# A hybrid decoder block: layer norm's sums kept group by group while the convolution runs

## The chip, the cores and the metric

The kernel runs on one core of a Trainium2 chip. The metric is the time of one execution on the device, in microseconds (us); lower is better. The kernel before took 1765.69 us, the median of three runs (1760.31 to 1766.15).

The core's engines run side by side, each working through its own queue in order: TensorE (PE, matmuls), VectorE (DVE), ScalarE (ACT), GpSimd (POOL) and SyncE (SP, which here only issues DMAs). An instruction that waits holds up whatever stands behind it in its queue.

## The reference

One decoder block over 256 positions of 2048 channels, all in float32. The part that the change touches is the causal convolution branch:

```python
def layernorm(x, g, b):
    mu = jnp.mean(xf, axis=-1, keepdims=True)
    var = jnp.mean(jnp.square(xf - mu), axis=-1, keepdims=True)
    y = (xf - mu) * lax.rsqrt(var + EPS) * g + b
...
def conformer_conv(glu_in, w_dw, b_dw, ln_g, ln_b, w_pw, b_pw):
    a, g = jnp.split(glu_in, 2, axis=-1)
    u = a * jax.nn.sigmoid(g)
    u = causal_dwconv(u, w_dw, b_dw)          # 31 taps, each channel alone
    u = jax.nn.silu(layernorm(u, ln_g, ln_b)) # over the 2048 channels
    return u @ w_pw + b_pw
...
proj = h @ w_in[l]                            # queries, keys, values, GLU input, merge gates
merged = jax.nn.sigmoid(ga) * y_a + jax.nn.sigmoid(gb) * y_b
x = x + g1 * (merged @ w_out[l])              # g1: a third of c_act @ w_ada's adaLN rows
```

Behind it stand a gated MLP and a final norm.

## The kernel before

**Weights and matmuls.** Every product streams its weights as tiles of 128x1024 (`wtile`): one DMA into `raw`, a rounded copy `hi` by ACT (L227), the remainder `lo` by DVE (L228). The pools hold four `raw` and three `hi` and `lo`, so `lo` of tile k can only be made once the matmuls of tile k-3 are over. A tile gives 12 matmuls of 512 columns (L249 to L251) in the products that this text speaks of. The tiles are counted here from 1 through the program: 187 to 218 are the merge gates of the convolution branch (`C_MB`), 219 to 250 the pointwise product `conv_pw_w`, which needs the whole normalised convolution `uT`, and 251 to 282 the product `w_out`.

**The convolution.** `u` holds the 2048 channels as 16 blocks of 128 (channels on partitions, 256 positions side by side). `conv_blocks` works on groups of 3, 3, 3, 3, 3 and 1 blocks: a tap is either one DVE instruction on one block (L549) or a product by ACT (L559) that DVE adds for the whole group (L568); the last tap writes the group back into `u` (L566). The running sum is the tile `cacc`, of which the pool holds two.

**Layer norm.** Sums over channels are sums over blocks (DVE) and then a matmul with ones (PE), which leaves the same sum on every partition. `ln_mean1` to `ln_mean4` add up all blocks, `ln_centre` subtracts the mean from four blocks at a time, squares them (ACT) and adds the squares up, `ln_var` makes 1/sqrt(variance) (one matmul, a square root on ACT, six small DVE instructions), `ln_scale` multiplies, `ln_silu` applies gain, bias and SiLU (ACT, block by block), `ln_split` makes `hi` and `lo` of the result for the matmuls (L350 on ACT, L351 on DVE).

**The adaLN rows.** `c_act @ w_ada` is done on DVE, one step (L298 or L301, on a tile of 128x1024 that has its own DMA, `araw`, two buffers) for each 128 rows. The 32 steps for `g1` are put in the queue by `conv_done`, when the convolution's pool is given back; `w_out`'s results need them. Others (`shift` and `scale` of the MLP) wait in the same queue.

**What sets the order.** Three queues of closures, `heads_q`, `conv_q` and `ada_q`, are dealt out by `tick` at each weight tile, by estimated loads; `norm_only` keeps `ada_q` back as long as `conv_q` still has steps. `drain(conv_q)` (L961) empties it when the gates' product has been issued. A scheduler then fixes each engine's order. All of that happens when the program is built.

## Time and profile before

| | |
|---|---|
| median of three runs | 1765.69 us (1760.31 to 1766.15) |
| the profiled execution | 1763.86 us, its span 1762.1 us |
| mean granted TensorE clock | 0.983 of full speed |
| busy: PE, DVE, ACT, POOL | 96%, 75%, 56%, 0% of the span |
| HBM traffic | 403.85 MB read, 2.10 MB written |

The span is what the profiler's records cover; the execution's own time is 1.8 us longer. A busy share is a mean over stages with different limits, and PE's is taken with matmul ends that are modelled: a full row says that matmuls followed each other without a gap. What a change in one stage is worth is read there, from which wait ends last. A wait is put down to the instruction whose end released it.

### The profile page before, as it was taken

How to read it: one execution, taken by the hardware profiler on the slowest of the kernel's cores; microseconds unless marked ns; L12 is line 12 of the kernel's file. 1: busy time of each engine (PE TensorE's matmuls, PEld its weight loads, DVE VectorE, ACT ScalarE, POOL GpSimd, SP SyncE). 2: the span in 40 equal slices, each digit the busy share in tenths (PEclk: the TensorE clock that was granted, in tenths of full speed). 3: DMA queues.
4: the chain of work that ended last, by engine and by line, in shares of the span. 5: the costliest groups of instructions: out<-in, count | busy, mean ns of one | idle time of the engine just before them, and what ended most of it. 6: DMA issues, size and time to landing. Idle time of an engine off the chain costs nothing.

```text
span 1762.1 us, 26526 instructions
## 1 busy us (share of the span) xinstructions
PE 1696.0 (96%) x10148; PEld 1468.2 (83%) x10148; DVE 1315.4 (75%) x1722; ACT 992.1 (56%) x1506; POOL 6.2 (0%) x28
## 2 busy tenths in 40 slices
PE   6999999999999999987999899999999999999997
PEld 4899999999887778865877888888988888898886
DVE  2677698898878899988897677776577776576665
ACT  4443576885677778755344565554455554345553
POOL 0000000000000000000000000000000000000000
PEclk8999999999999999998999999999999999999998
DMA  9999788877557346778898577776677765566653
GB/s 342 321 352 321 233 276 273 269 249 215 178 163 245 131 150 209 238 227 279 312 315 298 180 229 225 221 223 221 223 225 222 220 215 180 191 191 189 189 191 124
DMA packets 264362, 407.68 MB, mean 231 GB/s; under 512 B 12684, under 2 KB 156844, under 8 KB 263596
## 3 DMA queue, kind: packets, MB, share of 16 engines
q1 hardware_dynamic: 261676, 399.44, 69.9%
q10 hardware_dynamic: 2560, 6.55, 1.1%
q8 instruction: 79, 1.29, 0.3%
q14 instruction: 47, 0.39, 0.1%
HBM read 403.85 MB, written 2.10 MB: 230 GB/s over the span
## 4 chain that ended last, share of the span: by engine, by line
PE 87%; DMA 5%; DVE 4%; ACT 2%; issue 2%; SPq 0%; ACTq 0%; DVEq 0%
PE accp L282 18%; PE accx L250 12%; PE accx L249 11%; PE accx L251 11%; PE accp L283 9%; PE accw L261 6%; PE accw L264 6%; PE accw L263 6%; DMA araw<-in_w_ada_dram 3%; DVE t L301 1%; PE pt L788 1%; DVE lo L228 1%; PE pt L421 1%; PE pt L827 1%; DMA araw<-in_w_kc_dram 1%
## 5 line engine op out<-in xcount | busy, mean ns | idle before, releaser
L227 ACT CAST hi<-raw 128x1024 fp32r<-128x1024 f32 x546 | 572.1, 1048 | 639.7 <-PE accx L251 266.7
L228 DVE TENSOR_TENSOR lo<-raw,hi 128x1024 fp32r<-128x1024 f32 x546 | 665.5, 1220 | 317.8 <-ACT hi L227 314.3
L282 PE MATMUL accp<-act,hi 128*128 128x512 f32 x1408 | 495.5, 397 | 0.2
L249 PE MATMUL accx<-hi,act 128*128 128x512 f32 (+2 forms) x1176 | 429.1, 366 | 18.3 <-ACT act L350 17.7
L250 PE MATMUL accx<-lo,act 128*128 128x512 f32 (+2 forms) x1176 | 435.0, 370 | 3.9 <-DVE lo L228 3.7
L251 PE MATMUL accx<-hi,act 128*128 128x512 f32 (+2 forms) x1176 | 429.3, 365 | 0.8 <-DVE act L351 0.8
L283 PE MATMUL accp<-act,lo 128*128 128x256 f32 x1408 | 395.2, 281 | 0.2 <-DVE lo L228 0.2
L282 PEld LDWEIGHTS accp<-act,hi 128*128 128x128 f32 x1408 | 264.2, 188 | 64.1 <-DVE act L351 0.8
L249 PEld LDWEIGHTS accx<-hi,act 128*128 128x128 f32 x1176 | 222.8, 189 | 55.1 <-ACT act L350 18.6
L283 PEld LDWEIGHTS accp<-act,lo 128*128 128x128 f32 x1408 | 266.0, 189 | 0.8 <-DVE lo L228 0.6
L261 PE MATMUL accw<-act,hi 128*128 128x256 f32 x896 | 259.1, 290 | 4.9 <-ACT accw L587 2.8
L250 PEld LDWEIGHTS accx<-lo,act 128*128 128x128 f32 x1176 | 222.9, 190 | 45.3 <-DVE lo L228 9.7
L263 PE MATMUL accw<-act,hi 128*128 128x256 f32 x896 | 258.0, 288 | 0.0
L264 PE MATMUL accw<-act,lo 128*128 128x256 f32 x896 | 257.6, 288 | 0.2 <-DVE lo L228 0.2
L251 PEld LDWEIGHTS accx<-hi,act 128*128 128x128 f32 x1176 | 223.0, 190 | 36.7 <-issue 1.7
L261 PEld LDWEIGHTS accw<-act,hi 128*128 128x128 f32 x896 | 174.8, 195 | 11.7 <-issue 3.9
L264 PEld LDWEIGHTS accw<-act,lo 128*128 128x128 f32 x896 | 174.5, 195 | 3.9 <-issue 3.1
L263 PEld LDWEIGHTS accw<-act,hi 128*128 128x128 f32 x896 | 174.6, 195 | 3.5 <-issue 3.0
L301 DVE SCALAR_TENSOR_TENSOR t<-araw,cs,t 128x1024 f32<-128x1024 f32 x120 | 153.5, 1279 | 19.2 <-DMA araw<-in_w_ada_dram 18.9
L559 ACT ACTIVATE cprod<-big,cw 128x230 f32<-128x230 f32 (+27 forms) x298 | 124.6, 487 | 13.4 <-DVE cacc L568 11.3
L568 DVE TENSOR_TENSOR cacc<-cacc,cprod 128x726 f32<-128x726 f32 (+28 forms) x110 | 87.6, 797 | 11.4 <-ACT cprod L559 8.2
L549 DVE SCALAR_TENSOR_TENSOR cacc<-big,cw,cacc 128x232 f32<-128x232 f32 (+24 forms) x182 | 77.6, 463 | 0.6
(208 smaller groups left out, 1051.2 us busy)
## 6 DMA issues: line engine op xcount, KB each, us to landing
araw<-in_w_ada_dram SPq DMA_DIRECT2D x192, 512.0 KB, 5.0
raw<-in_w_in_dram SPq DMA_DIRECT2D x180, 512.0 KB, 4.9
raw<-in_ffn_w_up_dram SPq DMA_DIRECT2D x176, 512.0 KB, 4.5
raw<-in_ffn_w_down_dram SPq DMA_DIRECT2D x88, 512.0 KB, 3.7
raw<-in_w_o_nsa_dram SPq DMA_DIRECT2D x32, 512.0 KB, 3.7
raw<-in_conv_pw_w_dram SPq DMA_DIRECT2D x32, 512.0 KB, 5.6
raw<-in_w_out_dram SPq DMA_DIRECT2D x32, 512.0 KB, 5.2
araw<-in_w_kc_dram SPq DMA_DIRECT2D x8, 512.0 KB, 5.6
```

The source lines that it names most:

```text
L227: nc.scalar.copy(hi[:, :n], raw[:, :n])
L228: los.append(nc.vector.tensor_tensor(lo[:, :n], raw[:, :n], hi[:, :n], op=ALU.subtract).ins)
L249: nc.tensor.matmul(o, act[:, k, 0, s], hi, start=k == 0, stop=False)
L250: nc.tensor.matmul(o, act[:, k, 0, s], lo, start=False, stop=False)
L251: nc.tensor.matmul(o, act[:, k, 1, s], hi, start=False, stop=k == nk - 1)
L261: nc.tensor.matmul(acc[:, b, :], hi[:, s], act[:, k, 0, :], start=begin and k == first and b % 2 == 0, stop=False, skip_group_check=True)
L263: nc.tensor.matmul(acc[:, b, :], hi[:, s], act[:, k, 1, :], start=False, stop=False, skip_group_check=True)
L264: nc.tensor.matmul(acc[:, b, :], lo[:, s], act[:, k, 0, :], start=False, stop=last, skip_group_check=True)
L282: nc.tensor.matmul(acc[:, b], hi[:, s], act[:, k], start=k == 0, stop=False, skip_group_check=True)
L283: nc.tensor.matmul(acc[:, b, 0, :], lo[:, s], act[:, k, 0, :], start=False, stop=k == KB - 1, skip_group_check=True)
L301: nc.vector.scalar_tensor_tensor(acc, raw, cs[:, k:k + 1], acc, op0=ALU.mult, op1=ALU.add)
L559: nc.scalar.mul(box["p"][:, b - b0, s:], u[:, b, :T - s], cw[:, CW - 1 - s, b:b + 1])
```

## The change

The sums move into the convolution. After each group of `conv_blocks`, `norm_sums` subtracts a pivot from the group's blocks (`less`), squares them on ACT, and adds values and squares, 256 positions each, to the two halves of a tile `sq` (`add`). The pivot is the mean over the first group's 384 channels (`find`, once, with a matmul). At the end `ln_var` has one matmul with ones over both halves of `sq`: it makes the mean (less the pivot) and the variance as mean square less squared mean. `ln_scale` now subtracts the mean and multiplies. `ln_mean1` to `ln_mean4` and `ln_centre` are gone. `cacc` has one buffer where it had two, and the pool holds `sq` and `pivot` beside it. `norm_only` is set in `ln_var` and no longer in `conv_done`, which comes behind it; steps of `conv_q` that are dealt while it is set get a high priority, as those of `heads_q` have.

```diff
-            if q is heads_q:
+            if q is heads_q or q is conv_q and norm_only[0]:
                 es.enter_context(tc.high_priority(HP))
...
+    sq = cvp.tile([P, 2, T], F32, name="sq")
+    pivot = cvp.tile([P, T], F32, name="pivot")
+
+    def norm_sums(b0, n):
+        def sums(dst, a, fresh):
+            if fresh:
+                nc.vector.tensor_add(dst, a[:, 0, :], a[:, 1, :])
+            for j in range(2 if fresh else 0, n):
+                nc.vector.tensor_add(dst, dst, a[:, j, :])
+        def find():
+            sums(sq[:, 0, :], u[:, :n, :], True)
+            p_ = pt([P, T])
+            nc.tensor.matmul(p_, ones, sq[:, 0, :], start=True, stop=True)
+            nc.scalar.mul(pivot, p_, 1.0 / (n * P))
+        def less():
+            v = u[:, b0:b0 + n, :]
+            nc.vector.tensor_tensor(v, v, pivot[:, None, :].to_broadcast([P, n, T]), op=ALU.subtract)
+        def add():
+            v = u[:, b0:b0 + n, :]
+            s4 = t4([P, n, T])
+            nc.scalar.activation(s4, v, AF.Square)
+            sums(sq[:, 0, :], v, b0 == 0)
+            sums(sq[:, 1, :], s4, b0 == 0)
+        if b0 == 0:
+            conv_q.append(({"dve": 900, "act": 450, "pe": 250}, find))
+        conv_q.append(({"dve": 170 + n * 265}, less))
+        conv_q.append(({"dve": 840 * n, "act": 250 + 200 * n}, add))
...
-                    box["a"] = cvp.tile([P, n, T], F32, tag="cacc", name=nm("cacc"), bufs=2)
+                    box["a"] = cvp.tile([P, n, T], F32, tag="cacc", name=nm("cacc"))
...
+        norm_sums(b0, n)
...
     def conv_done():
         cv.__exit__(None, None, None)
-        norm_only[0] = True
...
     def ln_var():
+        norm_only[0] = True
+        vp = pt([P, 2, T])
+        nc.tensor.matmul(vp.rearrange("p a t -> p (a t)"), ones, sq.rearrange("p a t -> p (a t)"), start=True, stop=True)
         ve = t4([P, 4, T])
+        nc.vector.tensor_scalar(ve[:, 3, :], vp[:, 0, :], 1.0 / D, None, op0=ALU.mult)
+        nc.vector.tensor_mul(ve[:, 2, :], ve[:, 3, :], ve[:, 3, :])
+        nc.vector.scalar_tensor_tensor(ve[:, 0, :], vp[:, 1, :], 1.0 / D, ve[:, 2, :], op0=ALU.mult, op1=ALU.subtract)
+        nc.vector.tensor_scalar(ve[:, 0, :], ve[:, 0, :], EPS, None, op0=ALU.add)
...
     def ln_scale(j):
         def f():
             v = u[:, 4 * j:4 * j + 4, :]
+            nc.vector.tensor_tensor(v, v, lb["m"][:, None, :].to_broadcast([P, 4, T]), op=ALU.subtract)
             nc.vector.tensor_tensor(v, v, lb["r"][:, None, :].to_broadcast([P, 4, T]), op=ALU.mult)
...
+    conv_q.append(({"dve": 5500, "act": 500}, ln_var))
+    conv_q.append(({}, conv_done))
     conv_q.extend(({"dve": d, "act": a}, f) for d, a, f in
-                  [(1130, 0, ln_mean1), (1130, 0, ln_mean2), (1130, 0, ln_mean3), (900, 0, ln_mean4)]
-                  + [(2000, 1050, ln_centre(j)) for j in range(4)] + [(3000, 1700, ln_var)]
-                  + [(1130, 0, ln_scale(0))]
-                  + [i for j in range(4) for i in [(1130, 0, ln_scale(j + 1))] * (j < 3)
-                     + [(0, LN_SILU, ln_silu(4 * j)), (0, LN_SILU, ln_silu(4 * j + 2))]])
+                  [i for j in range(4) for i in [(2260, 0, ln_scale(j))]
+                   + [(0, LN_SILU, ln_silu(4 * j)), (0, LN_SILU, ln_silu(4 * j + 2))]])
```

The order that the scheduler makes of it is read at three places, all on DVE. In the changed kernel the lines of `conv_blocks` and `ln_*` have moved: L583, L602 and L600 are L549, L568 and L566; L553 is `less`, L543 an addition of `add`, L926 and L927 are `ln_scale`.

The first place is the hand-over to the last group of the convolution (one block). Before, at tiles 196 to 198 (`cacc_6793` is the running sum of blocks 12 to 14, `cacc_7423` that of block 15):

```order
L228 TENSOR_TENSOR lo_7661<-raw_7659,hi_7660 128x1024
L301 SCALAR_TENSOR_TENSOR t_1138_7313<-araw_7708,cs,t_1138_7313 128x1024
L568 TENSOR_TENSOR cacc_6793<-cacc_6793,cprod_7394 128x3x227
L568 TENSOR_TENSOR cacc_7423<-cacc_7423,cprod_7468 128x254
L228 TENSOR_TENSOR lo_7691<-raw_7689,hi_7690 128x1024
L566 TENSOR_TENSOR big_268<-cacc_6793,cprod_7417 128x768
```

and in the changed kernel, at tiles 208 to 210 (`cacc_7044` and `cacc_7739`):

```order
L228 TENSOR_TENSOR lo_7923<-raw_7921,hi_7922 128x1024
L602 TENSOR_TENSOR cacc_7044<-cacc_7044,cprod_7644 128x3x227
L600 TENSOR_TENSOR big_268<-cacc_7044,cprod_7667 128x768
L228 TENSOR_TENSOR lo_7953<-raw_7951,hi_7952 128x1024
L553 TENSOR_TENSOR big_268<-big_268,pivot 128x768
L228 TENSOR_TENSOR lo_7980<-raw_7978,hi_7979 128x1024
L301 SCALAR_TENSOR_TENSOR t_1132_7291<-araw_8030,cs,t_1132_7291 128x1024
L583 SCALAR_TENSOR_TENSOR cacc_7739<-big_268,cw,cacc_7739 128x250
```

The last group no longer starts beside the one in front of it, and the write-back of blocks 12 to 14 has moved from tile 197 to tile 208.

The second place is DVE's queue from `lo` of tile 221, the last that can be made ahead of the `conv_pw_w` product. Before (`t_1259_7920` is the tile in which `ln_var` works, `t_1296_8159` the sum of the first adaLN steps for `g1`; the row ahead of the first one is `lo` of tile 220 with L911 behind it):

```order
L228 TENSOR_TENSOR lo_8237<-raw_8235,hi_8236 128x1024
L914 TENSOR_TENSOR t_1259_7920<-t_1259_7920 128x256
L301 SCALAR_TENSOR_TENSOR t_1296_8159<-araw_8182,cs,t_1296_8159 128x1024
L915 TENSOR_TENSOR t_1259_7920<-t_1259_7920 128x256
L301 SCALAR_TENSOR_TENSOR t_1296_8159<-araw_8208,cs,t_1296_8159 128x1024
L916 TENSOR_SCALAR t_1259_7920<-t_1259_7920 128x256
L917 TENSOR_TENSOR t_1259_7920<-t_1259_7920 128x256
L923 TENSOR_TENSOR big_268<-big_268,t_1259_7920 128x1024 x4
```

and in the changed kernel (`cprod` are ACT's last products, `pt_8056` is the result of the one matmul):

```order
L228 TENSOR_TENSOR lo_8258<-raw_8256,hi_8257 128x1024
L602 TENSOR_TENSOR cacc_7739<-cacc_7739,cprod_7997 128x229
L602 TENSOR_TENSOR cacc_7739<-cacc_7739,cprod_8000 128x228
L602 TENSOR_TENSOR cacc_7739<-cacc_7739,cprod_8003 128x227
L600 TENSOR_TENSOR big_268<-cacc_7739,cprod_8006 128x256
L553 TENSOR_TENSOR big_268<-big_268,pivot 128x256
L543 TENSOR_TENSOR sq<-sq,big_268 128x256
L543 TENSOR_TENSOR sq<-sq,t_1279_8052 128x256
L911 TENSOR_SCALAR t_1281_8058<-pt_8056 128x256
L926 TENSOR_TENSOR big_268<-big_268,t_1281_8058 128x1024 x2
```

Behind these rows come L912, two more L926, L913 and L914, the reciprocal (L916), four small instructions (L917 to L920), the four L927 and the four L351; no L301 stands among them. The convolution's last four additions, its sums and all of `ln_var` have moved behind `lo` of tile 221. Before, the last write-back stood at tile 208 and the variance's matmul behind tile 218.

The third place is the product `w_out`, where the adaLN steps for `g1` end. Before, at tiles 259 to 262:

```order
L228 TENSOR_TENSOR lo_9156<-raw_9154,hi_9155 128x1024
L301 SCALAR_TENSOR_TENSOR t_1138_7313<-araw_9071,cs,t_1138_7313 128x1024
L228 TENSOR_TENSOR lo_9174<-raw_9172,hi_9173 128x1024
L1010 TENSOR_TENSOR t_1491_9143<-accx_8963,gb 128x512 x2
L301 SCALAR_TENSOR_TENSOR t_1138_7313<-araw_9074,cs,t_1138_7313 128x1024
L228 TENSOR_TENSOR lo_9192<-raw_9190,hi_9191 128x1024
```

and in the changed kernel, from tile 261 on (tiles 259 and 260 have two L301 each):

```order
L228 TENSOR_TENSOR lo_9223<-raw_9221,hi_9222 128x1024
L301 SCALAR_TENSOR_TENSOR t_1429_8890<-araw_8971,cs,t_1429_8890 128x1024
L301 SCALAR_TENSOR_TENSOR t_1429_8890<-araw_8974,cs,t_1429_8890 128x1024
L301 SCALAR_TENSOR_TENSOR t_1429_8890<-araw_8977,cs,t_1429_8890 128x1024
L228 TENSOR_TENSOR lo_9254<-raw_9252,hi_9253 128x1024
L301 SCALAR_TENSOR_TENSOR t_1132_7291<-araw_9053,cs,t_1132_7291 128x1024
L327 TENSOR_TENSOR gb<-pt_8981,gb 128x512
L327 TENSOR_TENSOR gb<-pt_8984,gb 128x512
L301 SCALAR_TENSOR_TENSOR t_1132_7291<-araw_9081,cs,t_1132_7291 128x1024
L351 TENSOR_TENSOR act_8216<-pt_9046,act_8216 128x2x256
L351 TENSOR_TENSOR act_8216<-pt_9074,act_8216 128x2x256
L301 SCALAR_TENSOR_TENSOR t_1132_7291<-araw_9102,cs,t_1132_7291 128x1024
```

The steps for `g1` begin behind `lo` of tile 230 instead of tile 220, and ten adaLN steps stand behind the four `lo` of tiles 259 to 262, where three stood. From tile 222 to tile 271 there are 41 steps, where there were 35.

## Rows read from the trace of the kernel before

**Rows 1.** The page's first part: span, busy time of each engine.

```profile
span 1762.1 us, 26526 instructions
...
PE 1696.0 (96%) x10148; PEld 1468.2 (83%) x10148; DVE 1315.4 (75%) x1722; ACT 992.1 (56%) x1506; POOL 6.2 (0%) x28
```

**Rows 2.** Stretches: us, PE, PEld, DVE, ACT, POOL busy (instructions), PEclk, DMA share, GB/s.

```profile
760.00:780.00 20.00, 20.00 (x89) 16.28 (x88) 17.80 (x22) 12.02 (x13) 0.00 (x0) 1.00 0.61 190
780.00:800.00 20.00, 4.58 (x21) 3.46 (x19) 16.58 (x18) 11.44 (x16) 0.00 (x0) 0.74 0.65 219
800.00:820.00 20.00, 18.02 (x67) 13.92 (x68) 16.93 (x15) 11.71 (x16) 0.00 (x0) 0.83 0.70 223
```

**Rows 3.** Timeline, PE: start, length, instruction [idle before].

```profile
784.19 0.39 PE L251 MATMUL accx<-hi,act 128*128 128x512 f32 x1
800.87 0.80 PE L249 MATMUL accx<-hi,act 128*128 128x512 f32 x1 [16.29 <-ACT act L350]
```

**Rows 4.** Timeline, DVE, the same stretch.

```profile
783.70 0.42 DVE L911 TENSOR_SCALAR t<-pt 128x256 f32<-128x256 f32 x1
...
785.92 1.75 DVE L913 RECIPROCAL t<-t 128x256 f32<-128x256 f32 x1 [1.14 <-ACT t L912]
...
790.80 1.28 DVE L301 SCALAR_TENSOR_TENSOR t<-araw,cs,t 128x1024 f32<-128x1024 f32 x1 [0.55 <-DMA araw<-in_w_ada_dram]
...
794.12 0.43 DVE L917 TENSOR_TENSOR t<-t 128x256 f32<-128x256 f32 x1
794.58 4.63 DVE L923 TENSOR_TENSOR big<-big,t 128x1024 f32<-128x1024 f32 x4
```

**Rows 5.** Timeline, ACT, the same stretch.

```profile
785.47 0.42 ACT L912 ACTIVATE t<-t 128x256 f32<-128x256 f32 x1
...
786.84 1.28 ACT L959 ACT_TABLE_LOAD   x1
788.13 1.02 ACT L959 ACTIVATE big<-accx 128x1024 f32<-128x1024 f32 x1
...
795.84 4.04 ACT L929 ACTIVATE big<-big,par 128x256 f32<-128x256 f32 x8 [5.39 <-DVE big L923]
799.78 1.03 ACT L350 CAST act<-big 128x1024 fp32r<-128x1024 f32 x1
```

**Rows 6.** Timeline, DVE, end of the convolution.

```profile
736.73 1.43 DVE L568 TENSOR_TENSOR cacc<-cacc,cprod 128x241 f32<-128x241 f32 x3
...
751.46 0.42 DVE L566 TENSOR_TENSOR big<-cacc,cprod 128x256 f32<-128x256 f32 x1
```

**Rows 7.** Timeline, ACT, end of the convolution.

```profile
738.17 1.26 ACT L559 ACTIVATE cprod<-big,cw 128x237 f32<-128x237 f32 x3
```

**Rows 8.** Timeline, PE, a 512-column float32 matmul with ones.

```profile
849.46 1.88 PE L326 MATMUL pt<-t,ones 128*128 128x512 f32 x4
```

**Rows 9.** Two more stretches, from the restart to w_out's second chunk.

```profile
815.50:951.30 135.80, 131.82 (x581) 104.39 (x579) 116.79 (x121) 53.70 (x59) 0.00 (x0) 1.00 0.92 324
816.00:830.00 14.00, 12.89 (x56) 10.11 (x55) 8.19 (x8) 4.21 (x4) 0.00 (x0) 1.00 1.00 378
```

**Rows 10.** DVE's groups there: busy us, mean ns, idle before, releaser.

```profile
L228 DVE TENSOR_TENSOR lo<-raw,hi 128x1024 fp32r<-128x1024 f32 x46 | 55.8, 1219 | 6.9 <-ACT hi L227 6.9
L301 DVE SCALAR_TENSOR_TENSOR t<-araw,cs,t 128x1024 f32<-128x1024 f32 x33 | 42.3, 1281 | 10.7 <-DMA araw<-in_w_ada_dram 10.7
```

**Rows 11.** Timeline, DVE: adaLN steps in and after the stop.

```profile
799.12 2.60 DVE L301 SCALAR_TENSOR_TENSOR t<-araw,cs,t 128x1024 f32<-128x1024 f32 x2
...
815.46 1.28 DVE L301 SCALAR_TENSOR_TENSOR t<-araw,cs,t 128x1024 f32<-128x1024 f32 x1
```

**Rows 12.** DMA issues there: KB each, median us to landing.

```profile
araw<-in_w_ada_dram SPq DMA_DIRECT2D x34, 512.0 KB, 5.2
```

**Rows 13.** Timeline, PE: a stop near 229 us.

```profile
229.13 0.39 PE L261 MATMUL accw<-act,hi 128*128 128x256 f32 x1 [2.76 <-ACT accw L587]
```

**Rows 14.** Timeline, PE: a stop near 610 us.

```profile
610.40 0.62 PE L822 MATMUL pt<-ident,s 128*128 128x128 f32 x2 [1.81 <-ACT s L817]
```

More of the change, by code (lines that the diff above doesn't have):

```diff
@@ L866, in conv_done @@
             ada_q.extendleft(reversed(ada_steps(2 * D + i * WT, to_bcast(gate1["b"], 2 * D, i), 1500)))
-    conv_q.append(({}, conv_done))
     lb = {}
-    def half_sum(dst, a):
-        nc.vector.tensor_add(a[:, 0:2, :], a[:, 0:2, :], a[:, 2:4, :])
-        nc.vector.tensor_add(dst, a[:, 0, :], a[:, 1, :])
-    def ln_mean1():
-        lb["a"] = t4([P, 4, T])
-        nc.vector.tensor_add(lb["a"], u[:, 0:4, :], u[:, 4:8, :])
-    def ln_mean2():
-        nc.vector.tensor_add(lb["a"], lb["a"], u[:, 8:12, :])
@@ L885, in ln_mean3 @@
-    def ln_mean3():
-        nc.vector.tensor_add(lb["a"], lb["a"], u[:, 12:16, :])
-    def ln_mean4():
-        half_sum(lb["a"][:, 0, :], lb["a"])
-        mp = pt([P, T])
-        nc.tensor.matmul(mp, ones, lb["a"][:, 0, :], start=True, stop=True)
-        lb["m"] = mp
-        lb["q"] = t4([P, 4, T])
-    def ln_centre(j):
-        def f():
-            v = u[:, 4 * j:4 * j + 4, :]
-            nc.vector.scalar_tensor_tensor(v, lb["m"][:, None, :].to_broadcast([P, 4, T]), -1.0 / D, v,
-                                           op0=ALU.mult, op1=ALU.add)
-            s4 = t4([P, 4, T])
-            nc.scalar.activation(s4, v, AF.Square)
-            half_sum(lb["q"][:, j, :], s4)
-        return f
@@ L905, in ln_var @@
     def ln_var():
-        q = lb["q"]
-        half_sum(q[:, 0, :], q)
-        vp = pt([P, T])
-        nc.tensor.matmul(vp, ones, q[:, 0, :], start=True, stop=True)
+        norm_only[0] = True
+        vp = pt([P, 2, T])
+        nc.tensor.matmul(vp.rearrange("p a t -> p (a t)"), ones, sq.rearrange("p a t -> p (a t)"), start=True, stop=True)
         ve = t4([P, 4, T])
-        nc.vector.tensor_scalar(ve[:, 0, :], vp, 1.0 / D, EPS, op0=ALU.mult, op1=ALU.add)
-        nc.scalar.activation(ve[:, 1, :], ve[:, 0, :], AF.Sqrt)
@@ L913, in ln_var @@
-        nc.vector.reciprocal(ve[:, 2, :], ve[:, 1, :])
-        nc.vector.tensor_mul(ve[:, 3, :], ve[:, 2, :], ve[:, 2, :])
-        nc.vector.tensor_mul(ve[:, 3, :], ve[:, 3, :], ve[:, 0, :])
-        nc.vector.tensor_scalar(ve[:, 3, :], ve[:, 3, :], -0.5, 1.5, op0=ALU.mult, op1=ALU.add)
-        nc.vector.tensor_mul(ve[:, 3, :], ve[:, 3, :], ve[:, 2, :])
-        lb["r"] = ve[:, 3, :]
+        nc.vector.tensor_scalar(ve[:, 3, :], vp[:, 0, :], 1.0 / D, None, op0=ALU.mult)
+        nc.vector.tensor_mul(ve[:, 2, :], ve[:, 3, :], ve[:, 3, :])
@@ new lines, in ln_var @@
+        nc.vector.scalar_tensor_tensor(ve[:, 0, :], vp[:, 1, :], 1.0 / D, ve[:, 2, :], op0=ALU.mult, op1=ALU.subtract)
+        nc.vector.tensor_scalar(ve[:, 0, :], ve[:, 0, :], EPS, None, op0=ALU.add)
+        nc.scalar.activation(ve[:, 2, :], ve[:, 0, :], AF.Sqrt)
+        nc.vector.reciprocal(ve[:, 1, :], ve[:, 2, :])
+        nc.vector.tensor_mul(ve[:, 2, :], ve[:, 1, :], ve[:, 1, :])
+        nc.vector.tensor_mul(ve[:, 2, :], ve[:, 2, :], ve[:, 0, :])
+        nc.vector.tensor_scalar(ve[:, 2, :], ve[:, 2, :], -0.5, 1.5, op0=ALU.mult, op1=ALU.add)
@@ L920, in ln_scale @@
+        nc.vector.tensor_mul(ve[:, 2, :], ve[:, 2, :], ve[:, 1, :])
+        lb["m"], lb["r"] = ve[:, 3, :], ve[:, 2, :]
     def ln_scale(j):
```

## The prediction

> **What bounds the kernel now.** I read the page's busy times first, then the span cut into stretches, then the timelines of PE, DVE and ACT where PE stops. PE is busy for 1696.0 of 1762.1 us [rows 1]: time comes or goes only where PE stops. In nearly all stretches it has 20.00 of 20 us, as from 760 to 780 [rows 2], 89 matmuls of 512 columns: 0.225 us each, 2.7 us for a weight tile's twelve. The one large stop lies at the change: 4.58 busy us from 780 to 800 at a granted clock of 0.74. PE issues the last matmul of the gates (tile 218) at 784.19 and the next (tile 219, which needs `uT`) at 800.87, idle for 16.29 us until ACT's first cast of `uT` [rows 3]. In between, DVE and ACT finish layer norm. The last DVE piece in front of SiLU is `ln_scale`, from 794.58 [rows 4]; ACT has waited 5.39 us for it when SiLU starts at 795.84, and PE starts 5.03 us after that [rows 3, 5].
>
> From there to 951 us PE loses another 4.0 us (131.82 of 135.80), in a stretch where the DMA engines are busy for 0.92 of the time and DVE for 116.79 us [rows 9]: the adaLN steps for `g1` share both with the weights. DVE waited 10.7 us there for their DMAs [rows 10].
>
> **What decides the change: where the convolution ends.** The second `cacc` is gone. Before, block 15's chain of 30 dependent taps ran beside blocks 12 to 14 and was written back at tile 208. Now it starts after them, with 2.7 us per tile of which `lo` takes 1.14 (four instructions of that size take 4.63 us [rows 4], so starts lie 1.14 apart); three taps take 1.43 [rows 6]. So three taps go with each tile and PE keeps its pace, but the last three land behind `lo` of tile 221. That `lo` cannot be made before the matmuls of tile 218 end, at 784.4. Hence the rest of the convolution and all of `ln_var` run while PE stands still, whatever the engines did earlier.
>
> **The stop, step by step**, with PE ending at 784.4 as before:
> - `hi` of tile 221 takes 1.05 on ACT and `lo` 1.14 on DVE, to 786.65. ACT makes the last gate (1.02 [rows 5]) and four products (1.26 for three [rows 7]): 788.15. The three additions and the write-back (0.42 [rows 6]) follow them: 788.75.
> - `less`, the addition of the values, ACT's square, the addition of the squares: 0.42 to 0.45 each, all dependent or nearly so: 790.1.
> - One matmul over 512 columns. Four records of that kind took 1.88 us, two for one matmul [rows 8]: 0.9 at the full clock. PE has then been idle for 5.7 us. After 16.29 idle us the first matmul took 0.80 where 0.39 is usual [rows 3], the lower level; so the bounds are 0.9 and 1.8. I take 1.7, as after the only long stop that I have a row of: 791.8.
> - L911 (0.34 to the next start), two subtractions of 1024, L912, two more subtractions, L913 and L914: 4 x 1.14 + 4 x 0.36 = 6.0, so 797.8. That is the order's doing: the four subtractions stand in front of the variance. The square root 0.5 [rows 5], the reciprocal 1.7 [rows 4], four small instructions at 0.42 on average (0.43 one, 0.46 to the next start [rows 4]): 801.7. The first L927 takes 1.26 until SiLU can start (794.58 to 795.84): 803.0.
> - From there 5.03 us to PE's first matmul: 808.0, against 800.87.
>
> So the stop grows by **7.1 us**; with the matmul at 0.9 it is 6.3. What falls away is in that: the variance's chain before took 12.1 us from L911 to SiLU (783.70 to 795.84), with three adaLN steps and 0.7 us of waits for their DMAs inside. The new one has none (4.3 us less), and the square root's table load can run beside the subtractions; but these are four more (4.6 us), and it starts 8.1 us later.
>
> On ACT one table load goes: the last gate now comes ahead of the square root. That load took 1.28 us, the gate started 0.01 us behind it, and ACT then waited 5.39 us for DVE [rows 5]: worth nothing. The Trainium skill ("ScalarE: Activation LUTs", What ACT_TABLE_LOAD costs) counts 1.28 us and a drain of 1.38 for every switch of table. By that the sum could be 2.7 us less if the switch lay on the path; the trace shows the load's 1.28 and no drain, and the wait behind it covers both.
>
> DVE instructions are counted above by their starts. The four of 1024 columns have a mean near 1.22 (as those of rows 10) and yet start 1.14 apart [rows 4]. The Trainium skill ("VectorE: DVE Perf Modes", The DRAIN you can't avoid) says that the next operation does not start until the pipeline is empty. Counting whole durations, the additional instructions of the stop would make it about 0.6 us longer; the rows do not bear it out, and the sum keeps the starts.
>
> **During the convolution** the change adds 30 additions of 256 positions (about 0.34) and five subtractions of 768 (about 0.85), 14.5 us; it takes away `ln_mean1` to `ln_mean4`, `ln_centre` and the first additions of `ln_var`, seven instructions of 1024 (1.14) and six pairs of 512 and 256 (about 0.6 and 0.34), 13.6 us. Until tile 218 that is the same DVE work, and ACT squares as much as before. PE's full stretches hide it (DVE at 17.80 of 20 [rows 2]); were the cover gone, the balance would cost 0.9 us. The pivot's matmul takes the place of the mean's, with as many columns. I take 0. What may shift are PE's stops of 2.76 and 1.81 us behind ACT [rows 13, 14]: bounds -5 and +5.
>
> **The adaLN steps behind the stop.** Before, eleven steps ran from 784 to 815.5, beside the stop. Now none does; two tiles are loaded and wait for tile 230. From tile 222 to 271 there are 41 steps instead of 35, none of them in the first eight tiles.
> - The worst place is tiles 259 to 262: ten steps behind four `lo`. With two `araw` buffers a step's DMA is issued only when the step two before it is done, and lands 5.2 us later [rows 12]. The seven steps from 799.12 to 815.46, which had nearly only themselves to wait for, lie 2.7 us apart on average [rows 11]. Ten at 2.7 are 27 us. PE has at most six tiles to run when the first is reached (three `lo` ahead, and those made in between): 16.3 us, and 2.6 for the matmuls with ones and the transposes there. It then waits 8 us. If the steps go at DVE's own 1.2 us they take 12 us, with four `lo` and four smaller instructions 19: no stop. At 3.1 us a step, with weights between: 12 us. Bounds 0 and 12; I take **8**, by the row of the steps themselves.
> - The other steps: four more DMAs of 0.52 MB than before, 2.1 MB. At the 324 GB/s of that stretch they take 6.5 us if nothing gives way, and nothing if the first eight tiles catch it: at 378 GB/s [rows 9] there is room. I take 2, nearer to the second, since those steps partly stand in the burst that I have counted.
> - What goes: between 816 and 830 PE lost 1.1 of 14.00 us at a DMA share of 1.00 [rows 9], when seven steps stood ahead of the weights of tile 226 in SP's queue. There is none there now. Minus **1**.
>
> SP's own issues are as many as before in all; for these steps it waits behind the same two buffers, and `raw` tiles queue behind them. That is in the 2.7 us.
>
> **The sum.** 7 + 0 + 8 + 2 - 1 = +16 us on the profiled execution of 1763.9 us (1762.1 of span and 1.8 around it): 1780. That execution lay 1.8 us below the median of 1765.7; I forecast **1782 us**.
>
> **Rivals.**
> - *The burst is hidden* (chance 0.19). The eight tiles without adaLN steps let `raw`, `hi` and `lo` run full, and PE eats the lead while DVE works through the ten steps. Then 8 and 2 are 0, and some of the 4.0 us lost before come back: 7 - 1 - 4 = +2 to +8, 1768 to 1774. For it: DVE's own 19 us are just what six tiles give. Against it: two `araw` buffers.
> - *DMA becomes the bound* from tile 230 on (0.22): one step and one weight tile per 2.7 us are 388 GB/s, more than the 378 reached in the fullest stretch. Then the burst costs 12, the other steps 6.5, with later weights besides: +24 to +30, 1790 to 1796.
> - *Faster* (0.04). The place is the stop: were the last products and taps done ahead of `lo` 221, as they were before, L911 would start about 784.5, SiLU 11.2 us later (the new chain's length), at 795.7 as now, and the stop would be no longer; with the convolution's stops gone (-5) and no burst, -9 us, 1757. It decides at whether a tap is done before 784.4; the order on DVE says no.
> - *The sums come no earlier* in effect, since the end of the convolution comes later: that is part of my forecast, and no case of its own.
>
> **How the numbers follow.** The forecast, 1775 to 1789, has 0.55. Its own spread: stop 6.3 to 8, burst 4 to 12, the rest 0 to 4. From 1768 to 1794 the range takes in the hidden burst and half of the DMA case, leaving out under 0.2. 0.5% (8.8 us, about what a measurement can tell from no change) ends at 1774.5: faster 0.04, same 0.18 (the hidden burst nearly whole), slower 0.78.
>
> **What the changed profile would show.** Right: one PE stop of 22 to 24 us ahead of L249's first matmul of `conv_pw_w`, released by ACT's cast; in it DVE's last L602, then L600, L553, two L543, L911, L926, no L301; a matmul with ones of 512 columns about 6 us into it; a second place of PE stops in `w_out`, some 110 to 120 us after the restart, released by `lo`, while DVE waits for `araw`. Wrong: PE's stop no longer than 16 us or the write-back of block 15 ahead of it; L301 closer than 2 us in the burst with PE full; a loss of more than 5 us ahead of 780 us.

## The result and the profile after

| | before | after |
|---|---|---|
| median | 1765.92 us (4 runs, 1760.31 to 1766.79) | 1786.97 us (4 runs, 1783.0 to 1793.28) |
| profiled execution; its span | 1763.86; 1762.1 us | 1784.92; 1782.5 us |
| mean granted TensorE clock | 0.983 | 0.975 |

The ratio is 1.0137, 95% interval 1.0099 to 1.0174: slower, by some 21 to 24 us. The forecast was 1782 us, in a range of 1768 to 1794.

The page's first part after, beside [rows 1]: DVE has 7.9 us more, PE 4.2 us, for the same 10148 matmuls.

```profile
span 1782.5 us, 26552 instructions
...
PE 1700.2 (95%) x10148; PEld 1471.9 (83%) x10148; DVE 1323.3 (74%) x1748; ACT 989.9 (56%) x1508; POOL 6.2 (0%) x28
```

Stretches of 20 us after (columns as in [rows 2]): the stop, and a second place that before does not have.

```profile
780.00:800.00 20.00, 6.56 (x22) 3.88 (x20) 15.82 (x26) 10.10 (x18) 0.10 (x1) 0.71 0.50 170
800.00:820.00 20.00, 11.16 (x41) 8.67 (x42) 13.96 (x15) 14.86 (x24) 0.00 (x0) 0.70 0.09 27
...
900.00:920.00 20.00, 17.75 (x76) 13.74 (x75) 18.25 (x20) 6.64 (x7) 0.00 (x0) 1.00 0.87 302
920.00:940.00 20.00, 14.22 (x41) 10.02 (x40) 12.62 (x11) 3.15 (x3) 0.00 (x0) 0.70 0.85 298
940.00:960.00 20.00, 14.05 (x49) 9.40 (x48) 12.34 (x13) 4.32 (x5) 0.00 (x0) 0.87 0.66 215
```

From 920 to 960 us PE runs 88 matmuls (two of those counted lie in both rows), where a full stretch has 89 in half that time, at a granted clock of 0.70 and 0.87.

**The stop.** PE's timeline after: the last gate matmul, the matmul with ones over the sums, the restart (before: [rows 3]).

```profile
784.10 0.39 PE L251 MATMUL accx<-hi,act 128*128 128x512 f32 x1
790.34 2.08 PE L909 MATMUL pt<-sq,ones 128*128 128x512 f32 x2 [5.85 <-DVE sq L543]
808.80 0.80 PE L249 MATMUL accx<-hi,act 128*128 128x512 f32 x1 [16.39 <-ACT act L350]
```

DVE's timeline in it, after, where [rows 4] had `ln_var` at its very start:

```profile
785.60 1.22 DVE L228 TENSOR_TENSOR lo<-raw,hi 128x1024 fp32r<-128x1024 f32 x1 [0.16 <-ACT hi L227]
786.90 1.40 DVE L602 TENSOR_TENSOR cacc<-cacc,cprod 128x229 f32<-128x229 f32 x3
788.43 0.43 DVE L600 TENSOR_TENSOR big<-cacc,cprod 128x256 f32<-128x256 f32 x1
...
792.45 0.42 DVE L911 TENSOR_SCALAR t<-pt 128x256 f32<-128x256 f32 x1 [2.17 <-PE pt L909]
792.91 2.36 DVE L926 TENSOR_TENSOR big<-big,t 128x1024 f32<-128x1024 f32 x2
...
798.24 0.29 DVE L914 TENSOR_SCALAR t<-t 128x256 f32<-128x256 f32 x1
...
802.51 4.63 DVE L927 TENSOR_TENSOR big<-big,t 128x1024 f32<-128x1024 f32 x4
```

and ACT's, from SiLU to the cast that PE waits for:

```profile
803.77 4.04 ACT L933 ACTIVATE big<-big,par 128x256 f32<-128x256 f32 x8 [3.48 <-DVE big L927]
807.72 1.03 ACT L350 CAST act<-big 128x1024 fp32r<-128x1024 f32 x1
```

The last taps stand behind `lo` of tile 221, as forecast. From the end of the gates to the restart it is 24.3 us (784.49 to 808.80), against 16.3.

**The second place.** DVE's timeline after, in w_out's first tiles, where the planner forces out what is left of `g1`'s steps:

```profile
936.15 2.61 DVE L301 SCALAR_TENSOR_TENSOR t<-araw,cs,t 128x1024 f32<-128x1024 f32 x2
942.45 1.23 DVE L228 TENSOR_TENSOR lo<-raw,hi 128x1024 fp32r<-128x1024 f32 x1 [3.69 <-ACT hi L227]
943.59 2.60 DVE L301 SCALAR_TENSOR_TENSOR t<-araw,cs,t 128x1024 f32<-128x1024 f32 x2
949.63 1.28 DVE L301 SCALAR_TENSOR_TENSOR t<-araw,cs,t 128x1024 f32<-128x1024 f32 x1 [3.44 <-DMA araw<-in_w_ada_dram]
```

and PE's timeline there:

```profile
925.27 0.51 PE L249 MATMUL accx<-hi,act 128*128 128x512 f32 x1 [1.14 <-ACT hi L227]
928.82 0.79 PE L250 MATMUL accx<-lo,act 128*128 128x512 f32 x1 [3.04 <-DVE lo L228]
...
951.06 2.75 PE L326 MATMUL pt<-t,ones 128*128 128x512 f32 x4 [2.92 <-DVE t L301]
```

Each link holds the next: `lo` stands behind steps that wait for their DMA, PE waits for `lo`, and the next `hi`, and `lo` with it, waits for PE to give a buffer back. Single stops are 0.5 to 3 us. From 900 to 920, with three of 0.5 to 1.2 us, the granted clock is still 1.00; behind the stop of 3.04 us, ahead of which PE had run one matmul since an idle 1.14, the records are at the lower level (0.79 us, as 0.80 behind the long stop in [rows 3]).

### The profile page after: what moved, and what is told of

Same layout as the page of the kernel before. It is cut to its first block, busy times and chain, and to the rows that moved or that the text cites. A ratio compares the mean times of both kernels' runs of the same rounds, so it can differ in the third digit from the quotient of the medians.

```text
span 1782.5 us, 26552 instructions
## 1 busy us (share of the span) xinstructions
PE 1700.2 (95%) x10148; PEld 1471.9 (83%) x10148; DVE 1323.3 (74%) x1748; ACT 989.9 (56%) x1508; POOL 6.2 (0%) x28
## 4 chain that ended last, share of the span: by engine, by line
PE 87%; DMA 5%; DVE 4%; ACT 2%; issue 1%; SPq 0%; DVEq 0%; ACTq 0%
PE accp L282 18%; PE accx L251 12%; PE accx L250 12%; PE accx L249 12%; PE accp L283 9%; PE accw L261 6%; PE accw L264 6%; PE accw L263 6%; DMA araw<-in_w_ada_dram 4%; PE pt L823 1%; DVE lo L228 1%; DVE t L301 1%; PE pt L421 1%; PE pt L862 1%; PE pt L671 0%
## 5 line engine op out<-in xcount | busy, mean ns | idle before, releaser
L249 PE MATMUL accx<-hi,act 128*128 128x512 f32 (+2 forms) x1176 | 432.2, 368 | 22.5 <-ACT act L350 17.9
L249 PEld LDWEIGHTS accx<-hi,act 128*128 128x128 f32 x1176 | 223.9, 190 | 62.8 <-ACT act L350 20.2
L301 DVE SCALAR_TENSOR_TENSOR t<-araw,cs,t 128x1024 f32<-128x1024 f32 x120 | 153.6, 1280 | 24.9 <-DMA araw<-in_w_ada_dram 24.8
L602 DVE TENSOR_TENSOR cacc<-cacc,cprod 128x726 f32<-128x726 f32 (+28 forms) x110 | 87.7, 797 | 13.4 <-ACT cprod L593 9.9
L583 DVE SCALAR_TENSOR_TENSOR cacc<-big,cw,cacc 128x232 f32<-128x232 f32 (+24 forms) x182 | 77.8, 462 | 0.5
```

The costliest lines, as they stand in the source:

```text
L249: nc.tensor.matmul(o, act[:, k, 0, s], hi, start=k == 0, stop=False)
L301: nc.vector.scalar_tensor_tensor(acc, raw, cs[:, k:k + 1], acc, op0=ALU.mult, op1=ALU.add)
```

## Where the time is, run by run

To compare all profiles I cut the span at three points of PE's timeline: the end of the gates (start of the last gate matmul and its 0.39 us), the restart (L249 behind ACT's cast), and the sublayer's end (the first transposition behind `w_out`, after a stop of 4.5 to 4.6 us in every profile). Steps are the L298 and L301 that DVE starts in the stop and behind it, up to the sublayer's end; the column "at 259" has those of them that stand on DVE behind `lo` of tile 259 and ahead of `lo` of tile 263, in `w_out`'s first tiles.

| profile | gates end | stop | restart to sublayer's end | PE idle in it | steps in stop, behind | at 259 | span |
|---|---|---|---|---|---|---|---|
| before | 784.6 | 16.3 | 200.7 | 4.9 | 5, 38 | 3 | 1762.1 |
| after | 784.5 | 24.3 | 216.8 | 14.4 | 0, 41 | 10 | 1782.5 |
| e1 before, one `cacc` | 788.9 | 19.8 | 198.3 | 4.4 | 7, 37 | 4 | 1764.3 |
| e2 no pivot | 786.7 | 15.0 | 210.2 | 11.0 | 0, 42 | 8 | 1775.1 |
| e3 account set back | 780.8 | 32.1 | 200.5 | 4.1 | 6, 35 | 5 | 1772.5 |
| e4 sums on GpSimd | 793.1 | 15.9 | 195.8 | 2.7 | 5, 35 | 3 | 1765.2 |
| e5 e3, steps behind norm | 783.0 | 24.3 | 204.6 | 7.9 | 2, 39 | 5 | 1771.2 |
| e6 e2, own `cacc` | 787.0 | 15.0 | 208.4 | 8.7 | 0, 42 | 8 | 1771.2 |
| e7 e5, small first | 780.6 | 20.6 | 208.8 | 10.1 | 1, 40 | 6 | 1772.8 |
| e8 combined | 786.3 | 10.7 | 207.5 | 10.3 | 1, 41 | 7 | 1764.2 |
| e9 after, due late | 783.2 | 24.3 | 193.5 | 0.3 | 0, 41 | 2 | 1760.5 |
| e10 combined, due late | 785.1 | 10.7 | 196.6 | 3.1 | 1, 41 | 3 | 1748.9 |
| e11 before, due late | 785.3 | 16.3 | 193.4 | 1.1 | 5, 38 | 3 | 1752.7 |

Behind the sublayer's end all run the same code, in 756.5 to 763.2 us. Up to the end of the gates after, e3, e5, e7 and e9 are the same program: 780.6 to 784.5 us. Differences of 4 us in these two parts are what single profiles scatter by. The length of the stretch in between goes with the steps at 259 (2 or 3 of them: 193.4 to 200.7 us; 10: 216.8), and not with all steps behind the restart: 41 of these are there in after, e8, e9 and e10, at 216.8, 207.5, 193.5 and 196.6 us.

## The experiments

e1 to e4, e5 to e8 and e9 to e11 ran together; ratios are to the kernel before in the same job (1761.65, 1761.11 and 1763.05 us). The changed kernel was not run again beside them, so that a comparison with it goes by the ratios.

**e1: before with one `cacc`.** The prediction put the late end of the convolution down to the missing buffer.

```diff
-    box["a"] = cvp.tile([P, n, T], F32, tag="cacc", name=nm("cacc"), bufs=2)
+    box["a"] = cvp.tile([P, n, T], F32, tag="cacc", name=nm("cacc"))
```

> The kernel before with a single cacc buffer, nothing else. Theory A (the missing buffer moves the end of the convolution, as the prediction said): block 15's taps start only after the write-back of blocks 12 to 14, its last taps land behind lo of tile 221, PE's stop ahead of L249 grows from 16.3 to 22 us or more, and the time is 6 us or more above before (about 1772). Theory B (the sums' DVE work, queued ahead of the later groups, moves it): with that work absent the write-back stays ahead of 780 us, the stop stays 16.3 +- 1 us, and the time is within 4 us of before.

Measured: 1763.77 us, ratio 1.0006 (0.9994 to 1.0019). DVE's timeline, block 15's write-back in e1 (751.46 in [rows 6]):

```profile
758.25 0.42 DVE L566 TENSOR_TENSOR big<-cacc,cprod 128x256 f32<-128x256 f32 x1
```

It stands 30.7 us ahead of the end of the gates, where before has 33.1. The stop is longer than theory B said, 19.8 us: five steps, with 2.7 us of waits for their DMAs (0.41, 1.32, 1.01), stand between the variance's instructions there. That is not A's mechanism. **Theory A, the cause that the prediction named, falls.**

**e2: after without the pivot.**

```diff
-        if b0 == 0:
-            conv_q.append(({"dve": 900, "act": 450, "pe": 250}, find))
-        conv_q.append(({"dve": 170 + n * 265}, less))
```

> After without the pivot: find and the five less are gone (two additions and five subtractions of up to 768, about 5 us of DVE); the variance is the mean of squares less the squared mean. One cacc buffer as in after. Theory B: 5 us at about 1.2 free DVE us per weight tile bring the end of the convolution 4 to 5 tiles forward, so block 15's write-back stands ahead of 784 us, the matmul of the sums runs between weight matmuls, and PE's stop shrinks from 24.2 to 12 to 16 us; with the adaLN burst still there the time is 8 to 13 us below after (1774 to 1779). Theory A: with one buffer the last taps stay behind lo of tile 221; only the last less (0.4 us) leaves the stop, which stays above 22 us, and the time is within 3 us of after.

Measured: 1771.27 us, ratio 1.0056 (1.0035 to 1.0078). The write-back in e2, on DVE, and the restart on PE:

```profile
774.96 0.43 DVE L596 TENSOR_TENSOR big<-cacc,cprod 128x256 f32<-128x256 f32 x1
```

```profile
801.67 0.80 PE L249 MATMUL accx<-hi,act 128*128 128x512 f32 x1 [15.02 <-ACT act L350]
```

The time is some 0.8% below after's by the ratios (1.0056 against 1.0137), 14 us, a little more than B said. Five us less of DVE work bring the write-back 13.5 us forward (788.43 in after). The sums were queued ahead of the later groups, and what DVE has free beside `lo` sets how fast the queue empties. The planner deals it by estimates (965 ns for `less` and 2520 for `add` of three blocks); e2 takes away the work and its estimate together, so that it does not part the two. Theory B holds, with one buffer.

**e6: e2 with a buffer of its own for block 15.**

```diff
-    box["a"] = cvp.tile([P, n, T], F32, tag="cacc", name=nm("cacc"))
+    box["a"] = cvp.tile([P, n, T], F32, tag="cacc" if n > 1 else "cacc1", name=nm("cacc"))
```

> e2 (after without the pivot) with a cacc buffer of its own for block 15, in the kilobyte that the pivot leaves. Theory B (queue): the convolution's pieces are taken from a first-in, first-out queue, so the buffer changes nothing: the write-back of block 15, the stop (15 us) and the time are those of e2 within 3 us. Theory A (buffer): block 15's chain runs beside blocks 12 to 14, its write-back stands 10 us or more earlier than in e2, and PE's stop is shorter by 3 us or more.

Measured: 1770.3 us, ratio 1.0052 (1.0036 to 1.0068), write-back at 775.27, the same stop of 15.0 us. The buffer changes nothing here either. No run has both the pivot and a second buffer.

**e3: the planner's account set back.** In after, `drain(conv_q)` charges DVE and ACT with what it empties, and `tick` then deals no adaLN step before tile 230.

```diff
     drain(conv_q)
+    for e in ("dve", "act", "dma"):
+        load[e] = min(load[e], load["pe"])
```

> After with the planner's account for DVE, ACT and DMA set back to PE's once the convolution's queue has been emptied, so that adaLN steps are dealt from tile 221 on, about one per tile, and no remainder is forced out at tiles 259 to 262. Theory C (the burst at the end costs the loss behind the stop): the stretch from PE's restart to the final reduce of the sublayer, 214.8 us in after and 198.7 in before, comes back to 198 to 204; the stop may grow by up to 4 us by steps that stand in it; time 8 to 14 us below after, 1773 to 1779. Theory D (DMA is the bound there: four more steps of 0.5 MB, whatever their order): the stretch stays above 210 us and the time within 4 us of after.

Measured: 1773.74 us, ratio 1.0072 (1.0052 to 1.0092). The stretch is what C said (200.5). The stop is 32.1 us, 7.8 more than in after, where C allowed 4. DVE's timeline in e3's stop, two of the six steps in it:

```profile
796.95 1.28 DVE L301 SCALAR_TENSOR_TENSOR t<-araw,cs,t 128x1024 f32<-128x1024 f32 x1 [0.76 <-DMA araw<-in_w_ada_dram]
...
805.35 1.28 DVE L301 SCALAR_TENSOR_TENSOR t<-araw,cs,t 128x1024 f32<-128x1024 f32 x1 [0.92 <-DMA araw<-in_w_ada_dram]
```

**e5: the same with the steps behind the norm's last multiplication**, by making them follow that instruction instead of an earlier `lo`; e3's edit stands.

```diff
+            lb["last"] = nc.vector.tensor_tensor(v, v, lb["r"][:, None, :].to_broadcast([P, 4, T]), op=ALU.mult).ins
...
+    los.extend([lb["last"]] * LAG)
```

> After with the account set back as in e3, and the adaLN steps dealt at tile 221 placed behind the last multiplication of layer norm (L929 of after's own numbering is unchanged in work). Theory C1 (in e3 the stop grew from 24.3 to 32.1 us because six steps and their DMA waits stood between the dependent instructions of the variance): from the last gate matmul to the restart it is 24 to 25.5 us again, the stretch behind it stays at 198 to 204 us, and the time is 4 to 9 us below e3, 14 to 19 below after, about 1767. Rival (the steps cost the same wherever they stand, because DVE and DMA have the same work): the stretch behind the stop grows by what the stop loses, and the time is within 3 us of e3.

Measured: 1769.55 us, ratio 1.0045 (1.003 to 1.006). The stop is after's 24.3 again, so C1 is right about it. But the stretch is 204.6 us, 4.1 above e3: half of what the stop gains (7.8) is given back, where the rival said all of it.

**e7: e5 with the variance's small instructions first.**

```diff
+            nc.vector.tensor_mul(ve[:, 3, :], ve[:, 3, :], ve[:, 2, :])
...
-            nc.vector.tensor_tensor(v, v, lb["m"][:, None, :].to_broadcast([P, 4, T]), op=ALU.subtract)
-            nc.vector.tensor_tensor(v, v, lb["r"][:, None, :].to_broadcast([P, 4, T]), op=ALU.mult)
+                if j:
+                    es.enter_context(tc.issue_after(lb["last"]))
+                nc.vector.tensor_tensor(v, v, lb["r"][:, None, :].to_broadcast([P, 4, T]), op=ALU.mult)
+                lb["last"] = nc.vector.tensor_tensor(v, v, lb["m"][:, None, :].to_broadcast([P, 4, T]), op=ALU.subtract).ins
+                lb.setdefault("first", lb["last"])
...
+    los.extend([lb["first"]] * LAG)
```

> e5 with the variance's small instructions in front of the four subtractions: the values are multiplied by r and then less m times r (one small multiplication more), group by group, and the adaLN steps stand behind the first group. Theory F (the order of four subtractions ahead of the variance costs the stop 3.4 us, less one more subtraction and one small instruction): from L911's counterpart to the first SiLU it takes 8.5 to 9 us instead of 11.3, the stop is 2 to 3 us shorter than in e5, and the time 1 to 4 us below e5. Rival (ACT's square root and table load set the pace, and DVE only waits): the stop is within 1 us of e5.

Measured: 1768.74 us, ratio 1.0046 (1.0029 to 1.0063). The stop is 3.7 us shorter than e5's, the stretch 4.2 longer, and the time that of e5. DVE's first small instruction, its reciprocal, ACT's SiLU and PE's restart in e7:

```profile
788.59 0.42 DVE L912 TENSOR_SCALAR t<-pt 128x256 f32<-128x256 f32 x1 [2.17 <-PE pt L909]
791.67 1.75 DVE L917 RECIPROCAL t<-t 128x256 f32<-128x256 f32 x1 [1.41 <-ACT t L916]
798.02 2.08 ACT L939 ACTIVATE big<-big,par 128x256 f32<-128x256 f32 x4 [5.08 <-DVE big L932]
801.23 0.79 PE L249 MATMUL accx<-hi,act 128*128 128x512 f32 x1 [12.68 <-ACT act L350]
```

Only half of the 3.7 us is F's. To SiLU it takes 9.43 us instead of 11.32 (F said 8.5 to 9), since the reciprocal now waits 1.41 us for ACT, whose table load no longer runs beside the subtractions (0.48 in after). The other half is a second effect of working group by group: ACT makes the first cast behind four blocks of SiLU (2.08 us), where after makes it behind eight (4.04), so that it takes 3.21 us from SiLU to the restart instead of 5.03.

**e8: all of it together**: the edits of e2, e3 and e7.

```diff
-        conv_q.append(({"dve": 170 + n * 265}, less))
...
+        load[e] = min(load[e], load["pe"])
+    los.extend([lb["first"]] * LAG)
```

> All that the theories B, C1 and F say together: no pivot (the sums ready before the stop), small instructions first, adaLN steps behind the first group of the norm, account set back. Expected: stop 11 to 13 us (16.3 in before, 24.3 in after), the stretch behind it 196 to 203 us, time 1754 to 1763, that is 0 to 0.5% below before. Rival: what the stop gives back the stretch behind it takes, because before did 11 adaLN steps beside its stop and this does 4: the stretch grows by 3 us or more and the time equals before.

Measured: 1763.6 us, ratio 1.0008 (0.9994 to 1.0022). The shortest stop so far (10.7 us, 5.6 less than in before), and the rival's result: the stretch is 6.8 us longer (207.5 against 200.7 in before). In e1 to e8 the stretch is 195.8 to 200.5 us with 35 to 37 steps behind the restart, and 204.6 to 210.2 with 39 to 42. Read so, a shorter stop was paid for with steps behind the restart. That led to e9. The column "at 259" of the table fits better: 7 steps stand there in e8, 3 in before.

**e9: after, with the steps due later.** `g1`'s first half is first needed behind `w_out`'s first chunk, its second half behind the third. The edit has three parts that no run takes apart: the first half now stands ahead of the second in the queue, each half has its own date, and a larger planned cost spaces the steps wider.

```diff
-        for i in range(2):
+        for i in (1, 0):
             ada_q.extendleft(reversed(ada_steps(2 * D + i * WT, to_bcast(gate1["b"], 2 * D, i), 1500)))
...
-    hurry = [(dict(cost, dma=1500), f) for cost, f in ada_q]
+    hurry = [(dict(cost, dma=2200), f) for cost, f in ada_q]
...
-    while len(ada_q) > gate1["rest"]:
-        ada_q.popleft()[1]()
+    def due(left):
+        while len(ada_q) > gate1["rest"] + left:
+            ada_q.popleft()[1]()
+
+    due(KB)
...
+        if i == 2:
+            due(0)
         residual(prod_x(mT, w_out, c0, w), c0, w, ss2, i)
```

> After with the adaLN steps of g1 forced out only where they are due: g1's first half (16 steps) before the first chunk of w_out, its second half before the third, instead of all before w_out; their planned DMA cost 2200 instead of 1500. The stop and the first step (tile 230) are as in after. Theory C2 (of the 16 us that the stretch behind the restart takes more than before, most is the forced remainder at tiles 259 to 262 and the clock that falls with it): the stretch goes from 216.8 to 200 to 207 us, no PE stop of over 2 us between 900 and 955 us, the time is 9 to 16 below after (1768 to 1775). Rival (the steps cost 2 us each wherever they go, since the stretch's length follows their number): 41 steps still behind the restart, stretch above 212 us, time within 4 us of after.

Measured: 1762.25 us, ratio 0.9994 (0.9978 to 1.0009): **with its stop of 24.3 us untouched, the changed kernel is back at the time of before**. The stretch is 193.5 us, shorter than C2 said and 7.2 us shorter than in before. PE's groups from 905 to 952 us, in after (busy us, mean ns | idle before, its releaser):

```profile
L250 PE MATMUL accx<-lo,act 128*128 128x512 f32 x36 | 16.7, 465 | 6.5 <-DVE lo L228 6.5
L249 PE MATMUL accx<-hi,act 128*128 128x512 f32 x36 | 16.2, 450 | 4.5 <-ACT hi L227 4.5
L251 PE MATMUL accx<-hi,act 128*128 128x512 f32 x36 | 16.0, 443 | 0.0
```

and in e9:

```profile
L249 PE MATMUL accx<-hi,act 128*128 128x512 f32 x69 | 26.8, 389 | 0.0
L250 PE MATMUL accx<-lo,act 128*128 128x512 f32 x68 | 26.5, 390 | 0.0
L251 PE MATMUL accx<-hi,act 128*128 128x512 f32 x68 | 26.5, 389 | 0.0
```

In the same 47 us PE does 108 of these in after and 205 in e9: 97 fewer at 0.225 us are 21.8 us. Some 14 are PE's waits (6.5 and 4.5, and 2.9 ahead of L326); most of the rest is the slower clock, whose mark is the mean of 443 to 465 ns instead of 389.

**e11: before, with the steps due later.** The edit of e9 alone, in before.

```diff
-    hurry = [(dict(cost, dma=1500), f) for cost, f in ada_q]
+    hurry = [(dict(cost, dma=2200), f) for cost, f in ada_q]
...
+    due(KB)
...
+            due(0)
```

> Before with the steps due as in e9, nothing else: its steps were never forced, so only their spacing changes. Expected: the stretch behind the restart falls from 200.7 to 195 to 199 us and the time by 0 to 5 us. If the time falls by as much as e10's, the norm's rearrangement has no part in what e10 gains.

Measured: 1754.68 us, ratio 0.9959 (0.9943 to 0.9974). The stretch falls to 193.4 us, e9's. As no step was forced in before, the dates have no part in this; the wider spacing or the order of the halves has. Both kernels now have the same stretch, so that e9 and e11 differ, but for scatter, by their stops alone: 8.0 us (24.3 and 16.3), and 7.6 us in the medians.

**e10: e8 with the steps due later**, by e9's edit.

```diff
-    hurry = [(dict(cost, dma=1500), f) for cost, f in ada_q]
+    hurry = [(dict(cost, dma=2200), f) for cost, f in ada_q]
...
+    due(KB)
...
+            due(0)
```

> e8 with the steps due as in e9. Theory: the stop stays at 10.7 us, the stretch behind it goes from 207.5 to 196 to 201 us; time 1752 to 1758, 0.2 to 0.6% below before. Rival: e8's loss is DMA and DVE work that only moves into w_out's second half, the time stays at 1761 to 1766.

Measured: 1750.8 us, ratio 0.9936 (0.9922 to 0.995): faster than before, after and e11. The restart on PE in e10:

```profile
795.79 0.79 PE L249 MATMUL accx<-hi,act 128*128 128x512 f32 x1 [10.68 <-ACT act L350]
```

Two thirds of the gain (8.4 of 12.3 us) e11 has without any change to the norm; the other 3.9 us come from e8's edits, those of the norm and the account: a stop 5.6 us shorter and a stretch 3.2 longer in the profiles.

**e4: after with the sums on GpSimd**, which is idle otherwise.

```diff
-                nc.vector.tensor_add(dst, dst, a[:, j, :])
+                nc.gpsimd.tensor_add(dst, dst, a[:, j, :])
...
-            nc.vector.tensor_tensor(v, v, pivot[:, None, :].to_broadcast([P, n, T]), op=ALU.subtract)
+            nc.gpsimd.tensor_tensor(v, v, pivot[:, None, :].to_broadcast([P, n, T]), op=ALU.subtract)
```

> After with the 30 additions of the sums and the five subtractions of the pivot on GpSimd instead of VectorE, with their DVE cost taken out of the planner's account. Theory B: the convolution's groups end as early as before (write-back ahead of 775 us), the sums and most of the variance are done ahead of PE's stop; what is left behind it is lo of tile 221, a few adaLN steps, the first multiplication, SiLU and the cast (5.03 us): stop 8 to 12 us, 4 to 8 below before; adaLN steps are dealt as before; time 1754 to 1764. Rival E (GpSimd slows VectorE beside it, or its additions of 256 take several us each, so that the convolution's groups wait for them): DVE's additions or lo get longer than 1.4 us, PE loses more than 5 us ahead of 780 us, or the last sum ends behind 786 us; time 1770 or more.

Measured: 1766.85 us, ratio 1.0032 (1.0021 to 1.0042). B is right that the convolution ends early again (write-back at 767.51), but the stop is 15.9, not 8 to 12: five steps stand in it, one with 2.41 us of waiting for its DMA. And E has its part: PE loses 8.8 us between 600 us and the end of the gates, against 3.6 in before. GpSimd's timeline in e4, at the end of a group:

```profile
736.88 1.84 POOL L553 TENSOR_TENSOR big<-big,pivot 128x768 f32<-128x768 f32 x1 [6.92 <-DVE big L600]
738.80 2.48 POOL L543 TENSOR_TENSOR sq<-sq,big 128x256 f32<-128x256 f32 x2
```

DVE's in the same 15 us:

```profile
737.32 2.49 DVE L228 TENSOR_TENSOR lo<-raw,hi 128x1024 fp32r<-128x1024 f32 x1 [0.58 <-ACT hi L227]
739.73 0.95 DVE L583 SCALAR_TENSOR_TENSOR cacc<-big,cw,cacc 128x250 f32<-128x250 f32 x1
740.61 1.75 DVE L228 TENSOR_TENSOR lo<-raw,hi 128x1024 fp32r<-128x1024 f32 x1
...
749.04 0.45 DVE L583 SCALAR_TENSOR_TENSOR cacc<-big,cw,cacc 128x232 f32<-128x232 f32 x1
...
750.54 1.23 DVE L228 TENSOR_TENSOR lo<-raw,hi 128x1024 fp32r<-128x1024 f32 x1
```

Beside GpSimd `lo` takes 2.49 and 1.75 us instead of 1.23, a tap 0.95 instead of 0.45.

## Why the prediction was right, and where not

**The stop: right, 8.0 us for 7.1.** The write-back ends at 788.86 (forecast 788.75). The matmul with ones came out slower than its upper bound of 1.8: 2.11 us from its start to L911, and L911 at 792.45, where the step said 1.7 and 791.8. From L911 to SiLU it is 11.32 us (forecast 11.2), and from there to the restart 5.03, as in before. That the stop pays for the four subtractions in front of the variance, e7 shows: with the small instructions first SiLU starts 1.9 us sooner behind L911 (the other 1.8 us of its shorter stop are ACT's earlier cast).

**Its cause: wrong.** "The second `cacc` is gone" was the step, and e1 and e6 show that the buffer hardly moves the end. What moves it is the DVE work that stands ahead of the later groups in a first-in, first-out queue. The prediction weighed this work against what the change removes (14.5 against 13.6 us) and found nothing lost. The balance was right and the order not: what it removes came behind the convolution, what it adds comes ahead of its end. In e2 some 5 us of this work are worth 13.5 us of delay; at that rate 14.5 us are 39, an estimate, and the write-back is 37 us later (751.46 to 788.43). I had read the late taps from the order and given them the nearest reason, so the right length of the stop is no proof of the cause.

**The convolution's stage: nothing to see.** The gates end at 784.5 and 784.6. The five profiles of this program scatter over 3.9 us, so a gain of 2 us could not be told.

**The adaLN steps: mis-sized.** The terms 8, 2 and -1 make +9; the stretch is 16.1 us longer. PE's idle time grows by 9.5 (14.4 against 4.9), which is what the terms counted. The remaining 6.6 are matmuls at the lower clock: from 928.2 to 941.8 and from 952.1 to 955.5 us the granted clock is 0.50 and PE busy for 14.3 us, half of which, 7.2, is the price of that level; right behind the restart it costs 1.6, 1.0 less than in before. The step took the price of a stop to be its length. That all of it is the steps' doing, e9 shows: with as many of them, but 2 instead of 10 at tiles 259 to 262, the stretch is 193.5 us.

**The sum.** Forecast 1780 us for the profiled execution, measured 1784.9: stop +0.9, steps +7.1, the part behind the sublayer -3.6 (scatter), the time around the span +0.6; with the gates 0.1 earlier that is 4.9. The scatter hid half of what the steps' term missed; that the total came so near is in part luck.

**The rivals.** *Hidden burst*: no, PE has 14.4 us of stops. *DMA the bound*: e9 carries the same steps and weights and PE waits 0.3 us, so the total traffic is not what binds; how the steps are crowded is. *Faster* was to decide at whether the last taps are done before 784.4: in e2 they are, and the stop is 15.0 us, no longer than before, as that rival said.

The Trainium skill ("ScalarE: Activation LUTs", What ACT_TABLE_LOAD costs) adds a drain to a table load. In e8's profile a load of 1.28 us starts at 784.77 and the square root behind it at 786.06, 0.01 us after its end; the load for the last gate starts at 787.48, 0.02 us behind the cast in front of it, and the gate at 788.77. The trace shows no drain of 1.38 us at either.

**What stays open:** by what means crowded steps cost PE time, whether by DVE's own time, the two `araw` buffers or the DMA queue. Nor is it shown which part of e9's edit does it. In before, and behind e3's edit, which e8 has too, no step is forced out, and yet the edit takes 7.3 us from before's stretch and 10.9 from e8's: there it is not the dates. Nor is it explained why the same code behind the sublayer takes 756.5 in one profile and 763.2 in another.

## What to carry to other kernels

Work that is moved into an earlier stage is not hidden by that stage's average slack: look where it stands in the queue, and divide it by what is free per step there. When a planner has a hard date, look at what a shift does to what has to be out by then: here ten steps piled up in front of a date that stood ahead of their first use, and later dates with a wider spacing gave the changed kernel back all that the change had cost it. Look at the spacing even where no date presses: the same edit took 8.4 us off the kernel before. And price stops of a few us on TensorE with the clock that follows them, not with their length alone.
